# Turning more activations with transposing transfers instead of TensorE, in a two-layer hybrid encoder on one core

## The chip, the cores and the metric

The kernel runs on one core of a Trainium2 chip. The metric is the device time of one execution in microseconds (us). Three runs of the kernel before took 907.43, 908.38 and 909.86 us; the median is 908.38 us. The profile comes from a further execution, which took 909.68 us.

## The reference

The program is an encoder trunk of two layers for one sequence of 256 tokens and a width of 1024, in float32. Each layer projects the normalized input once and feeds two branches; their gated sum goes through an output projection, a SwiGLU feed-forward block and a per-layer embedding. Cut to what matters here:

```python
def hybrid_layer(h, p_i, ...):
    u = rms_norm(h, g_mix_pre)
    (gq, gk, gv, gg, ra_f, ra_b, aq, ak, av, gate_a, gate_b) = jnp.split(u @ w_in, offsets, axis=-1)
    ...                                       # gated linear attention, both directions
    o_gla = rms_norm(o_f + o_b, g_gla_out).reshape(b, s, GLA_VAL)
    branch_a = (o_gla * jax.nn.silu(gg)) @ w_o_gla          # the gated outputs
    q = apply_axial_rope(rms_norm(aq.reshape(b, s, ATTN_HEADS, HEAD_DIM), g_q_norm), cos, sin)
    k = apply_axial_rope(rms_norm(ak.reshape(b, s, ATTN_KV_HEADS, HEAD_DIM), g_k_norm), cos, sin)
    branch_b = gqa_attention(q, k, v) @ w_o_attn            # 8 query heads in 2 groups
    mixed = jax.nn.sigmoid(gate_a) * branch_a + jax.nn.sigmoid(gate_b) * branch_b   # the mix
    h = h + rms_norm(mixed @ w_out, g_mix_post)
    gate, up = jnp.split(rms_norm(h, g_ffn_pre) @ w_ffn_in, 2, axis=-1)
    h = h + rms_norm((jax.nn.silu(gate) * up) @ w_ffn_out, g_ffn_post)              # hidden: 2816
    e = p_i @ w_ple_proj
    return h + rms_norm(jax.nn.sigmoid(h @ w_ple_gate) * e, g_ple_post)
```

## The kernel before

**Products in three passes.** Every float32 operand of a product is kept as a high part and a low part in the type fp32r, and a product is three passes on TensorE (PE): high by high, low by high, high by low. `split` makes the parts: a CAST on ScalarE (ACT) for the high part, a subtraction on VectorE (DVE) for the low part (both are line 134 of the profile).

**Weights.** They stream from HBM by transfers that SyncE (SP) issues, 1 MB at a time into a `raw` or `lent` buffer. ACT casts each to `wh` in two pieces of 128x1024, DVE makes `wl` from `raw` and `wh`, and PE reads the two. A raw buffer is free for the next load when DVE is through with it.

**Activations.** The tokens stand in two halves of 128 (`hf`). A result that is the next product's contracted operand has to be turned, 128x128 at a time. There are two ways to do it.

- `transpose_in` (and, with code of its own, the queries' loop in `attend`, line 1267): PE transposes four blocks against `ident` into a bank of PSUM (`aux`), then `split` reads the bank. The profile shows these transposes as matmuls of 128x128 with `ident`.
- `turn_out` and `take_in`: ACT copies a 128x512 float32 tile as 16-bit words, the low and the high words apart (line 468), SP issues a transposing transfer of the words (DMA_TRANSPOSE, line 469), and ACT copies the turned words together again (line 476), after which `split` reads them from SBUF. The kernel before does this for all hidden blocks of the feed-forward block but the last pair, nine transfers per layer.

**The order.** Work beside the main run of products is written as generators in a `Task`. Each `yield n` asks to be called again after n ticks, and each half of a projection's product is a tick. `WAIT_MIX`, `W["g"]` and `WAIT_TURNED` are such counts. Inside `tc.high_priority(AHEAD)` instructions are placed ahead of their place in the code, as early as their operands allow. Each engine then works its own list in order: an instruction that waits holds up all behind it on its engine.

**Where the turned tiles occur.** In `attend(g)` for g = 0 and g = 1 each half of the queries (`qrs`, in the profile `mid_0rq` and `mid_1rq`, the digit being the layer) is transposed, scores against the keys follow, then softmax. The keys' parts lie in `big_0kv` and are made by the same casts and subtractions. In `out_gate` the gated outputs (`mid_0gg`) become `gT` (`big_0gg`). In `merge` the sum of the gated branches (`big_0gate`, by half `hf` and column half `j`) becomes `mixT` (`big_0merge`), read by the product with `w_out` (`acc_0wout`). `turn_in`, used by `out_gate`, makes a task that calls `transpose_in` twice for each half.

Of the kernel before, what the change touches and what calls it, by code (L numbers as in the profile page):

```python
# [13 lines left out]
U16 = mybir.dt.uint16  # L14
# [4 lines left out]
P = 128  # L19
T = 256  # L20
# [12 lines left out]
W = dict(r=5, z=6, s0=4, s=3, s1=9, o0=1, o=1, k=4, q=3, a0=1, a1=4, a2=4, a3=1, g=6)  # L33

STEPS_FIRST = "00 10 01 11 02 12 03 13".split()
STEPS = "00 01 02 10 03 11 12 13".split()
# [24 lines left out]
def trunk_kernel(ctx: ExitStack, tc: tile.TileContext, a: dict, out: bass.AP):  # L61
# [7 lines left out]
    nc = tc.nc  # L69
# [11 lines left out]
    part = ["start"]  # L81
# [8 lines left out]
    def mid(dt=F32):  # L90
        return b4p.tile([P, 1024], dt, tag="mid", name=nm("mid"))
# [4 lines left out]
    def aux():  # L96
        return accp.tile([P, 512], F32, tag="acc", name=nm("aux"))
# [34 lines left out]
    def split(hi, lo, src):  # L132

        return nc.scalar.copy(hi, src), nc.vector.tensor_tensor(out=lo, in0=src, in1=hi.bitcast(F32), op=ALU.subtract)  # L134


    h = cp.tile([P, 2, D], F32, tag="h", name="h")
# [24 lines left out]
    ident = cp.tile([P, P], F32, tag="ident", name="ident")  # L162
# [282 lines left out]
    def transpose_in(sp, src, k, n, hf, plain=None):  # L445

        ps = aux()
        for i in range(n):
            nc.tensor.transpose(ps[:, i * P : (i + 1) * P], src[:, i * P : (i + 1) * P], ident)
        with tc.high_priority(AHEAD):  # L450
            sp.put(ps[:, : n * P], k, n, hf * P, P)
        if plain is not None:
            nc.scalar.copy(plain, ps[:, : n * P])

    def turn_out(src, k, hf):

        with tc.high_priority(AHEAD):
            both, turned = halves(mid())
            turned = turned.bitcast(U16)
            parts = both.bitcast(U16).rearrange("p (s c) -> p s c", s=2)  # L460
            words = src.bitcast(U16)
            if hf is None:
                nc.scalar.copy(
                    parts.rearrange("p s (k h f) -> p s k h f", k=2, f=P),
                    words.rearrange("p (h k f s) -> p s k h f", h=2, f=P, s=2),
                )
            else:
                nc.scalar.copy(parts, words.rearrange("p (c s) -> p s c", s=2))
            nc.sync.dma_start_transpose(out=turned.rearrange("p (x t) -> p x t", t=P), in_=parts.rearrange("p s c -> p (s c)"))
        return both, turned  # L470

    def take_in(sp, both, turned, k, hf):

        n, tn = (2, T) if hf is None else (4, P)
        hi, lo = sp.at(k, n, (hf or 0) * P, tn)
        nc.scalar.copy(
            both.bitcast(U16).rearrange("p (k t s) -> p k t s", s=2, t=tn),
            turned.rearrange("p (s k t) -> p k t s", s=2, t=tn),
        )
        split(hi, lo, both.rearrange("p (k t) -> p k t", t=tn))  # L480

    last_pow = [None]

# [62 lines left out]
    def halves(t):  # L546
        return [t[:, j * 512 : (j + 1) * 512] for j in range(2)]

    def turn_in(sp, x, hf, wait, plain=None, apart=False):


        def turn():
            yield wait
            for j, y in enumerate(halves(x)):
                if j and apart:
                    yield 1
                transpose_in(sp, y, 4 * j, 4, hf, plain and plain[j])

        sp.makers[hf].append(Task(turn(), part[0]))
# [489 lines left out]
    for l in range(DEPTH):  # L1049
# [58 lines left out]
        qrs, qss, ranks = [], [], []  # L1108
# [50 lines left out]
        o = {}  # L1159
# [100 lines left out]
        def attend(g):  # L1260
            qs = []
            for hf in range(2):
                yield W["q"]
                ps = aux()
                for i in range(4):
                    hd = 4 * g + i
                    nc.tensor.transpose(ps[:, i * P : (i + 1) * P], qrs[hf][:, hd * P : (hd + 1) * P], ident)
                qh, ql = halves(mid(F32R))
                split(qh, ql, ps)
# [173 lines left out]
        gg = big().rearrange("p (s c) -> p s c", s=2)  # L1443
        for j in range(2):
            o = project(uT)
# [69 lines left out]
        def merge(br):  # L1515
            def then(j, hf, o):
                sl = [s[:, hf, j * 512 : (j + 1) * 512] for s in sgate[: br + 1]]
                vmul(sl[br], o, sl[br])
                if br == 1:
                    nc.vector.tensor_tensor(out=sl[0], in0=sl[0], in1=sl[1], op=ALU.add)  # L1520
# [46 lines left out]


        part[0] = f"{l}ffnin"
        hid = Split()  # L1570
        us = [[ws.take() for _ in range(2)] for _ in range(2)]

        def turned(src, k, hf):

            def turn():
                if k == 2 * PAIRS[-1]:
                    yield WAIT_LAST[hf]
                    transpose_in(hid, src, k, 4, hf)
                else:
                    x = turn_out(src, k, hf)  # L1580
                    yield WAIT_TURNED
                    take_in(hid, *x, k, hf)
# [193 lines left out]
```

## Time and profile before

| | |
|---|---|
| runs, us | 907.43, 908.38, 909.86 |
| profiled execution, us | 909.68 |
| its span, us | 907.9 |
| PE busy | 898.8 us, 99% |
| DVE busy | 790.2 us, 87% |
| ACT busy | 620.5 us, 68% |
| POOL busy | 105.9 us, 12% |
| weights' queue (q1) | 177.25 MB, 59.9% of the 16 DMA engines' span |
| clock granted to PE | 0.999 |

The span is what lies between the first and the last instruction of the profile; 1.8 us of the profiled execution's own time lie outside it. In a timeline row the first number is the start in us from the span's start, the second the time from the first start to the last end of a group, and a bracket at the end names idle time of the engine ahead of the group and what ended it. In rows of groups by line, three durations in ns are the least, the median and the longest. Times of single rows below are of this one execution.

### The profile page before, as it was taken

To read this page: it belongs to the slowest core of one execution; us is meant where nothing else is said; L and a number is where in the kernel's file an instruction comes from. 1 tells how busy PE (TensorE), PEld (TensorE's weight loads), DVE (VectorE), ACT (ScalarE), POOL (GpSimd) and SP (SyncE) were. 2 spreads that over 40 slices of the span, in tenths; PEclk is the share of its full clock that TensorE was granted. 3 is DMA by queue.
4 is the path that set the end of the run, shared out by engine and by line. 5 is a ranking of instruction groups with operands and counts; after the bars stand their busy time and mean duration, and the time that the engine had idled before them with its cause. 6 is when DMAs were issued, how large, how long until landed. Compare 5 with 4: busy or idle time off the path is not lost.

```text
span 907.9 us, 12157 instructions
## 1 busy us (share of the span) xinstructions
PE 898.8 (99%) x4479; PEld 762.2 (84%) x4479; DVE 790.2 (87%) x1021; ACT 620.5 (68%) x1011; POOL 105.9 (12%) x157
## 2 busy tenths in 40 slices
PE   9999999999999999999999999999999999999997
PEld 8898888888888887887898888888888888888886
DVE  7999989987668999998779899799876799999984
ACT  7688677564467787756676687675644796958563
POOL 3700221300100000000254001110000000000001
PEclk9999999999999999999999999999999999999999
DMA  8663445657397594956576424455573966858461
GB/s 283 219 189 136 140 140 191 216 187 249 115 288 204 173 301 146 317 170 233 180 279 204 168 93 140 139 186 185 186 241 100 309 180 206 254 210 264 150 231 47
DMA packets 108519, 178.16 MB, mean 196 GB/s; under 512 B 22494, under 2 KB 46566, under 8 KB 107948
## 3 DMA queue, kind: packets, MB, share of 16 engines
q1 hardware_dynamic: 108300, 177.25, 59.9%
q8 instruction: 35, 0.57, 0.3%
q14 instruction: 24, 0.20, 0.1%
q10 hardware_dynamic: 160, 0.14, 0.0%
HBM read 169.50 MB, written 3.15 MB: 190 GB/s over the span
## 4 chain that ended last, share of the span: by engine, by line
PE 78%; DVE 11%; DMA 4%; issue 4%; ACT 2%; POOL 0%; SPq 0%; POOLq 0%; ACTq 0%; DVEq 0%
PE acc_1ffnin L122 12%; PE acc_0gate L122 7%; PE acc_1gate L122 7%; PE acc_1ffnin L106 7%; DVE wl_0ffnin L134 6%; PE acc_1rq L122 3%; PE acc_0gqk L106 2%; PE acc_1gqk L106 2%; PE acc_1wout L122 2%; PE acc_0ple L122 2%; PE acc_1v L122 2%; PE acc_0gg L122 2%; PE acc_1gg L122 2%; PE acc_0v L122 2%; PE acc_0merge L122 2%
## 5 line engine op out<-in xcount | busy, mean ns | idle before, releaser
L134 ACT CAST wh_0ffnin<-raw_0ffnin 128x1024 fp32r<-128x1024 f32 x38 | 38.1, 1048 | 19.8 <-DMA raw_0ffnin<-in_w_ffn_out_dram 10.2
L134 ACT CAST wh_1ffnin<-raw_1ffnin 128x1024 fp32r<-128x1024 f32 x38 | 38.3, 1048 | 17.4 <-DMA raw_1ffnin<-in_w_ffn_out_dram 5.0
L134 DVE TENSOR_TENSOR wl_0ffnin<-raw_0ffnin,wh_0ffnin 128x1024 fp32r<-128x1024 f32 x38 | 44.6, 1219 | 5.8 <-ACT wh_0ffnin L134 5.8
L134 DVE TENSOR_TENSOR wl_1ffnin<-raw_1ffnin,wh_1ffnin 128x1024 fp32r<-128x1024 f32 x38 | 44.8, 1219 | 5.0 <-ACT wh_1ffnin L134 4.9
L106 PE MATMUL acc_0ffnin<-wh_0ffnin,big_0ffnin 128*128 128x512 f32 x176 | 45.4, 392 | 0.0
L106 PE MATMUL acc_1ffnin<-wh_1ffnin,big_1ffnin 128*128 128x512 f32 x176 | 45.1, 390 | 0.0
L122 PE MATMUL acc_0ffnin<-wh_0ffnin,big_0wout 128*128 128x512 f32 x168 | 41.8, 390 | 0.0
L122 PE MATMUL acc_1ffnin<-wh_1ffnin,big_1wout 128*128 128x512 f32 x168 | 41.5, 389 | 0.0
L106 PEld LDWEIGHTS acc_0ffnin<-wh_0ffnin,big_0ffnin 128*128 128x128 f32 x176 | 32.8, 188 | 7.5 <-DVE big_0ffnin L134 0.5
L106 PEld LDWEIGHTS acc_1ffnin<-wh_1ffnin,big_1ffnin 128*128 128x128 f32 x176 | 33.0, 188 | 6.9
L122 PEld LDWEIGHTS acc_0ffnin<-wh_0ffnin,big_0wout 128*128 128x128 f32 x168 | 31.4, 188 | 7.1 <-ACT wh_0ffnin L134 0.4
L122 PEld LDWEIGHTS acc_1ffnin<-wh_1ffnin,big_1wout 128*128 128x128 f32 x168 | 31.5, 188 | 6.5
L134 DVE TENSOR_TENSOR wl_1ffnin<-lent_1ffnin,wh_1ffnin 128x1024 fp32r<-128x1024 f32 x30 | 35.7, 1217 | 0.6 <-ACT wh_1ffnin L134 0.6
L134 DVE TENSOR_TENSOR wl_0ffnin<-lent_0ffnin,wh_0ffnin 128x1024 fp32r<-128x1024 f32 x30 | 35.6, 1216 | 0.1
L134 ACT CAST wh_1ffnin<-lent_1ffnin 128x1024 fp32r<-128x1024 f32 x30 | 30.7, 1051 | 5.4 <-PE acc_1ffnin L106 3.9
L134 ACT CAST wh_0ffnin<-lent_0ffnin 128x1024 fp32r<-128x1024 f32 x30 | 30.4, 1053 | 3.6 <-DVE lent_0ffnin L332 3.4
L134 ACT CAST wh_0gate<-raw_0gate 128x1024 fp32r<-128x1024 f32 x20 | 19.9, 1049 | 14.4 <-DMA raw_0gate<-in_w_o_attn_dram 6.1
L134 ACT CAST wh_1gate<-raw_1gate 128x1024 fp32r<-128x1024 f32 x20 | 19.9, 1048 | 13.9 <-PE acc_1gate L122 5.9
L134 DVE TENSOR_TENSOR wl_0gate<-raw_0gate,wh_0gate 128x1024 fp32r<-128x1024 f32 x20 | 24.2, 1257 | 5.2 <-ACT wh_0gate L134 5.1
L134 DVE TENSOR_TENSOR wl_1gate<-raw_1gate,wh_1gate 128x1024 fp32r<-128x1024 f32 x20 | 23.5, 1221 | 5.1 <-ACT wh_1gate L134 5.1
L106 PE MATMUL acc_0ffnin<-wl_0ffnin,big_0ffnin 128*128 128x512 f32 x88 | 24.6, 394 | 0.6 <-DVE wl_0ffnin L134 0.6
L106 PE MATMUL acc_1ffnin<-wl_1ffnin,big_1ffnin 128*128 128x512 f32 x88 | 24.0, 391 | 0.0
(730 smaller groups left out, 2731.7 us busy)
## 6 DMA issues: line engine op xcount, KB each, us to landing
raw_0ffnin<-in_w_ffn_out_dram SPq DMA_DIRECT2D x11, 1024.0 KB, 5.9
raw_1ffnin<-in_w_ffn_out_dram SPq DMA_DIRECT2D x11, 1024.0 KB, 5.5
lent_0ffnin<-in_w_ffn_in_dram SPq DMA_DIRECT2D x6, 1024.0 KB
lent_1ffnin<-in_w_ffn_in_dram SPq DMA_DIRECT2D x6, 1024.0 KB, 7.5
raw_0v<-in_w_in_dram SPq DMA_DIRECT2D x4, 1024.0 KB, 5.8
raw_0gate<-in_w_o_gla_dram SPq DMA_DIRECT2D x4, 1024.0 KB, 6.8
raw_0gate<-in_w_o_attn_dram SPq DMA_DIRECT2D x4, 1024.0 KB, 5.2
raw_0wout<-in_w_ffn_in_dram SPq DMA_DIRECT2D x8, 512.0 KB, 4.6
```

Source lines behind the costliest of these rows:

```text
L106: return nc.tensor.matmul(o, lhsT, rhs, start=start, stop=stop)
L122: nc.tensor.matmul(o, x, y, start=start and n == 0, stop=stop and n == len(seq) - 1, **kw)
L134: return nc.scalar.copy(hi, src), nc.vector.tensor_tensor(out=lo, in0=src, in1=hi.bitcast(F32), op=ALU.subtract)
```

## The change

Three more kinds of tile go the second way, in each of the two layers: the queries of the second group (g = 1; two tiles, 8 PE transposes), the gated outputs (four tiles, 16 transposes), and the mix apart from the tile of the second column half and first token half (three tiles of four, 12 of 16 transposes). So 36 PE transposes per layer go, and 9 transposing transfers with two ACT copies each come.

`turn_out` no longer takes a buffer of its own: one half buffer that is free by then (`parts`) takes the words apart, and the transfer writes the turned words back over the source. For the queries, `parts` is the half that held the first group's queries, so the first copy comes after that group's PE transposes. The transfer is issued outside `high_priority`, which holds for the feed-forward block's nine transfers per layer, too. The counts of ticks change: `WAIT_GATED` = 9, 11 replaces `W["g"]` = 6, and `WAIT_MIX` is counted by `j` and `hf`.

```diff
-WAIT_MIX = 3, 6
+WAIT_MIX = (5, 7), (3, 8)
...
+WAIT_GATED = 9, 11
...
-    def turn_out(src, k, hf):
+    def turn_out(src, parts, mixed=False):
         with tc.high_priority(AHEAD):
-            both, turned = halves(mid())
...
+            planes, words = (t.bitcast(U16) for t in (parts, src))
...
-                nc.scalar.copy(parts, words.rearrange("p (c s) -> p s c", s=2))
-            nc.sync.dma_start_transpose(out=turned.rearrange("p (x t) -> p x t", t=P), in_=parts.rearrange("p s c -> p (s c)"))
-        return both, turned
+                nc.scalar.copy(planes.rearrange("p (s c) -> p s c", s=2), words.rearrange("p (c s) -> p s c", s=2))
+        nc.sync.dma_start_transpose(out=words.rearrange("p (x t) -> p x t", t=P), in_=planes)
...
+                if g == 0:
+                    ps = aux()
+                    for i in range(4):
+                        nc.tensor.transpose(ps[:, i * P : (i + 1) * P], qrs[hf][:, i * P : (i + 1) * P], ident)
+                    split(qh, ql, ps)
+                else:
+                    take_in(*(t.rearrange("p (i t) -> p i t", t=P) for t in (qh, ql)), *halves(qrs[hf])[::-1])
...
                 prs.append(softmax(g, hf, qs[hf]))
+                if g == 0:
+                    turn_out(*halves(qrs[hf])[::-1])
...
-                turn_in(gT, sg, hf, W["g"])
+                xs = [(t, gg[:, hf, j * 512 : (j + 1) * 512]) for j, t in enumerate(halves(sg))]
+                for x in xs:
+                    turn_out(*x)
+                def turn(hf=hf, xs=xs):
+                    for j, x in enumerate(xs):
+                        yield WAIT_GATED[hf] if j == 0 else 1
+                        take_in(*gT.at(4 * j, 4, hf * P, P), *x)
...
                     def turn():
-                        yield WAIT_MIX[hf]
-                        transpose_in(mixT, sl[0], 4 * j, 4, hf)
+                        if (j, hf) != (1, 0):
+                            turn_out(*sl)
+                        yield WAIT_MIX[j][hf]
+                        if (j, hf) != (1, 0):
+                            take_in(*mixT.at(4 * j, 4, hf * P, P), *sl)
+                        else:
+                            transpose_in(mixT, sl[0], 4 * j, 4, hf)
```

In layer 0 the start of the attention shows what this does to ACT's list. `mid_0at` are the first group's queries, turned; `big_0kv` the keys; `wh_0kv` high parts of weights. Before:

```order
L134 CAST mid_0at_673<-aux_0at_668 128x512
L134 CAST wh_0kv_570<-raw_0rq_423 128x1024
L499 ACTIVATE big_0kv_539<-acc_0kv_541,rs_start_121 128x256
L1194 ACTIVATE t_0kv_610<-t_0kv_610,kss_0kv_611 128x128
L1194 ACTIVATE t_0kv_624<-t_0kv_624,kss_0kv_625 128x128
L1194 ACTIVATE t_0kv_610<-t_0kv_610,kss_0kv_611 128x128
L1194 ACTIVATE t_0kv_624<-t_0kv_624,kss_0kv_625 128x128
L134 CAST wh_0kv_570<-raw_0rq_423 128x1024
L134 CAST big_0kv_539<-aux_0kv_684 128x2x128
L134 CAST mid_0at_710<-aux_0at_705 128x512
L134 CAST big_0kv_539<-aux_0kv_713 128x2x128
```

The same stretch of ACT's list in the changed kernel:

```order
L466 COPY mid_0rq_161<-mid_0rq_161 128x1024
L135 CAST mid_0at_668<-aux_0at_669 128x512
L135 CAST wh_0kv_570<-raw_0rq_423 128x1024
L495 ACTIVATE big_0kv_539<-acc_0kv_541,rs_start_121 128x256
L1190 ACTIVATE t_0kv_610<-t_0kv_610,kss_0kv_611 128x128
L1190 ACTIVATE t_0kv_624<-t_0kv_624,kss_0kv_625 128x128 x2
L1190 ACTIVATE t_0kv_610<-t_0kv_610,kss_0kv_611 128x128
L135 CAST wh_0kv_570<-raw_0rq_423 128x1024
L466 COPY mid_0rq_163<-mid_0rq_163 128x1024
L135 CAST wh_0kv_602<-raw_0rq_528 128x1024 x2
L135 CAST big_0kv_539<-aux_0kv_684 128x2x128
L135 CAST mid_0at_705<-aux_0at_706 128x512
```

A first copy of words stands ahead of the first queries' cast, and a second copy and two casts of `wh_0kv_602` now stand ahead of both casts of the keys; before, the casts of `wh_0kv_602` followed the keys. The second cast of `big_0kv` is the next row after these.

On PE, the end of the first product block of `gqk` and the first scores (`aux_0at` out of `big_0kv` and `mid_0at`), before:

```order
L106 MATMUL acc_0gqk_642<-big_start_303,wh_0rq_522 128x512 x4
L106 MATMUL acc_0gqk_642<-big_start_303,wl_0rq_523 128x256 x4
L106 MATMUL aux_0at_727<-big_0kv_539,mid_0at_673 128x256
L106 MATMUL acc_0gqk_643<-big_start_303,wh_0rq_522 128x512
L106 MATMUL aux_0at_743<-big_0kv_539,mid_0at_673 128x256
L106 MATMUL acc_0gqk_643<-big_start_303,wh_0rq_522 128x512 x3
L106 MATMUL acc_0gqk_643<-big_start_303,wl_0rq_523 128x256 x4
```

And in the changed kernel:

```order
L107 MATMUL acc_0gqk_642<-big_start_303,wh_0rq_522 128x512 x4
L107 MATMUL acc_0gqk_642<-big_start_303,wl_0rq_523 128x256 x4
L107 MATMUL acc_0gqk_643<-big_start_303,wh_0rq_522 128x512 x4
L107 MATMUL acc_0gqk_643<-big_start_303,wl_0rq_523 128x256 x4
L107 MATMUL aux_0at_727<-big_0kv_539,mid_0at_668 128x256
L107 MATMUL aux_0at_743<-big_0kv_539,mid_0at_668 128x256
L107 MATMUL acc_0gqk_785<-big_start_149,wh_0kv_570 128x512 x2
```

The first two scores moved behind the eight matmuls into `acc_0gqk_643`.

At the end of the mix, ACT's list before (`big_0merge` is the turned mix, `aux_0merge` the PSUM bank that PE's transposes write):

```order
L134 CAST big_0merge_2215<-aux_0merge_2244 128x4x128
L134 CAST wh_0merge_2267<-raw_0merge_2188 128x1024 x2
L134 CAST big_0merge_2327<-aux_0merge_2322 128x4x128
L134 CAST mid_0wout_2301<-aux_0emb_2330 128x512
L524 ACTIVATE t_0wout_2377,ss_0wout_2375<-acc_0wout_2302 128x512
L134 CAST big_0merge_2327<-aux_0merge_2355 128x4x128
```

And in the changed kernel:

```order
L135 CAST big_0merge_2222<-big_0gate_2040 128x4x128
L135 CAST wh_0merge_2253<-raw_0merge_2180 128x1024 x2
L466 COPY big_0gate_2040<-big_0gate_1718 128x1024
L135 CAST big_0merge_2313<-aux_0merge_2308 128x4x128
L135 CAST mid_0wout_2287<-aux_0emb_2316 128x512
L472 COPY big_0gate_2040<-big_0gate_1718 128x1024
L135 CAST big_0merge_2313<-big_0gate_2040 128x4x128
```

The copy for the mix's last tile now stands between the casts of the weights and the cast of the one tile that PE still transposes.

More of the change, by code (lines that the diff above doesn't have):

```diff
@@ L30 @@
 WAIT_NEXT, WAIT_IN, WAIT_H = (7, 9), ((6, 9), (6, 6)), ((3, 5), (3, 5))
-WAIT_MIX = 3, 6
+WAIT_MIX = (5, 7), (3, 8)
 WAIT_SPREAD = 12
-W = dict(r=5, z=6, s0=4, s=3, s1=9, o0=1, o=1, k=4, q=3, a0=1, a1=4, a2=4, a3=1, g=6)
+W = dict(r=5, z=6, s0=4, s=3, s1=9, o0=1, o=1, k=4, q=3, a0=1, a1=4, a2=4, a3=1)
+WAIT_GATED = 9, 11
 STEPS_FIRST = "00 10 01 11 02 12 03 13".split()
@@ L453, in transpose_in @@
             nc.scalar.copy(plain, ps[:, : n * P])
-    def turn_out(src, k, hf):
+    def turn_out(src, parts, mixed=False):
         with tc.high_priority(AHEAD):
-            both, turned = halves(mid())
[L459 to L462, printed above, removed]
+            planes, words = (t.bitcast(U16) for t in (parts, src))
+            if mixed:
                 nc.scalar.copy(
-                    parts.rearrange("p s (k h f) -> p s k h f", k=2, f=P),
+                    planes.rearrange("p (s k h f) -> p s k h f", s=2, k=2, f=P),
                     words.rearrange("p (h k f s) -> p s k h f", h=2, f=P, s=2),
@@ L467, in turn_out, with take_in @@
             else:
-                nc.scalar.copy(parts, words.rearrange("p (c s) -> p s c", s=2))
-            nc.sync.dma_start_transpose(out=turned.rearrange("p (x t) -> p x t", t=P), in_=parts.rearrange("p s c -> p (s c)"))
-        return both, turned
-    def take_in(sp, both, turned, k, hf):
-        n, tn = (2, T) if hf is None else (4, P)
-        hi, lo = sp.at(k, n, (hf or 0) * P, tn)
+                nc.scalar.copy(planes.rearrange("p (s c) -> p s c", s=2), words.rearrange("p (c s) -> p s c", s=2))
+        nc.sync.dma_start_transpose(out=words.rearrange("p (x t) -> p x t", t=P), in_=planes)
+    def take_in(hi, lo, src, parts):
+        tn = hi.shape[-1]
         nc.scalar.copy(
-            both.bitcast(U16).rearrange("p (k t s) -> p k t s", s=2, t=tn),
-            turned.rearrange("p (s k t) -> p k t s", s=2, t=tn),
+            parts.bitcast(U16).rearrange("p (k t s) -> p k t s", s=2, t=tn),
+            src.bitcast(U16).rearrange("p (s k t) -> p k t s", s=2, t=tn),
         )
-        split(hi, lo, both.rearrange("p (k t) -> p k t", t=tn))
+        split(hi, lo, parts.rearrange("p (k t) -> p k t", t=tn))
     last_pow = [None]
@@ L1263, in attend @@
                 yield W["q"]
[L1264 to L1267, printed above, removed]
                 qh, ql = halves(mid(F32R))
-                split(qh, ql, ps)
+                if g == 0:
[5 more added lines that the diff above has]
+                    take_in(*(t.rearrange("p (i t) -> p i t", t=P) for t in (qh, ql)), *halves(qrs[hf])[::-1])
                 qs.append((qh, ql, qss[hf][:, 4 * g : 4 * g + 4]))
@@ L1461, in out_gate @@
                     vmul(t, t, on[:, hf, s])
-                turn_in(gT, sg, hf, W["g"])
+                xs = [(t, gg[:, hf, j * 512 : (j + 1) * 512]) for j, t in enumerate(halves(sg))]
[5 more added lines that the diff above has]
+                        take_in(*gT.at(4 * j, 4, hf * P, P), *x)
+                gT.makers[hf].append(Task(turn(), part[0]))
         ogate = Task(out_gate(), f"{l}gg")
@@ L1569, in trunk_kernel @@
         part[0] = f"{l}ffnin"
-        hid = Split()
+        hid, spare = Split(), []
         us = [[ws.take() for _ in range(2)] for _ in range(2)]
@@ L1579, in turn @@
                 else:
-                    x = turn_out(src, k, hf)
+                    if not spare:
+                        spare.extend(halves(mid()))
+                    parts = spare.pop()
+                    turn_out(src, parts, hf is None)
                     yield WAIT_TURNED
-                    take_in(hid, *x, k, hf)
+                    take_in(*(hid.at(k, 2, 0, T) if hf is None else hid.at(k, 4, hf * P, P)), src, parts)
             t = Task(turn(), part[0], k // 4)
```

## The prediction

> **What bounds the kernel now.** I read the page's busy times first, then the chain that ended last, then timelines at the places that the change touches. From the page:
>
> ```profile
> span 907.9 us, 12157 instructions
> PE 898.8 (99%) x4479; PEld 762.2 (84%) x4479; DVE 790.2 (87%) x1021; ACT 620.5 (68%) x1011; POOL 105.9 (12%) x157
> PE 78%; DVE 11%; DMA 4%; issue 4%; ACT 2%; POOL 0%; SPq 0%; POOLq 0%; ACTq 0%; DVEq 0%
> ```
>
> PE is busy for 99% of the span and carries 78% of the last chain. So a PE instruction that goes is time that goes, provided that no operand of a later one comes late. DVE's 87% warns that there are stretches in which its products (the low parts) arrive just in time; the windows show them for the stages concerned:
>
> ```profile
> core 0: us, PE busy (x) PEld busy (x) DVE busy (x) ACT busy (x) POOL busy (x), PEclk, DMA share, GB/s
> 45.00:100.00 55.00, 55.00 (x319) 48.08 (x318) 52.41 (x94) 45.39 (x95) 7.04 (x6) 1.00 0.45 148
> 147.00:201.00 54.00, 54.00 (x248) 44.95 (x247) 50.74 (x48) 33.91 (x41) 10.47 (x10) 1.00 0.52 176
> 248.00:300.00 52.00, 51.64 (x230) 41.49 (x229) 40.42 (x48) 38.61 (x58) 2.01 (x5) 1.00 0.80 232
> ```
>
> The first row is the attention's start in layer 0, the second the stage that takes the gated outputs, the third the start of the feed-forward block. PE never rests in the first two, while DVE is at 52.41 of 55 and 50.74 of 54 us, and ACT at 45.39 of 55. ACT has room on the whole, but little in the first.
>
> **What PE gets back.** Three of the removed sets, from PE's timeline; a row's own length holds the drain of its last matmul, so I count from its start to the next row's start:
>
> ```profile
> 97.22 0.60 PE L1267 MATMUL aux_0at<-ident,mid_0rq 128*128 128x128 f32 x4
> 97.57 0.71 PE L122 MATMUL acc_0v<-wh_0v,big_start 128*128 128x512 f32 x2
> ...
> 147.70 1.91 PE L449 MATMUL aux_0gg<-ident,mid_0gg 128*128 128x128 f32 x16
> 149.36 0.70 PE L122 MATMUL acc_0gate<-wh_0gg,big_start 128*128 128x512 f32 x2
> ...
> 216.12 0.60 PE L449 MATMUL aux_0merge<-ident,big_0gate 128*128 128x128 f32 x4
> 216.47 0.71 PE L122 MATMUL acc_0merge<-wh_0gate,big_0at 128*128 128x512 f32 x2
> ```
>
> Four transposes push PE back by 0.35 us, sixteen by 1.66. Per layer: 2 x 0.35 for the queries, 1.66 for the gated outputs, 3 x 0.35 for the mix, together 3.41 us; in two layers **-6.8 us**. That is the most that the change can give directly.
>
> **What ACT and SP get.** The feed-forward block shows the price of the new pieces:
>
> ```profile
> L468 ACT COPY mid_0ffnin<-t_0ffnin x6: 1038/1044/1047, 267.2 to 376.0; 128x1024 uint16<-128x1024 uint16 x6
> L476 ACT COPY mid_0ffnin<-mid_0ffnin x9: 1168/1177/1183, 274.0 to 380.8; 128x1024 uint16<-128x1024 uint16 x9
> L469 SPq DMA_TRANSPOSE mid_0ffnin<-mid_0ffnin x9: 1237/1250/1922, 268.3 to 377.1; - x9
> DMA to landing us min/median/max: 3.3/3.6/4.3
>   DMA mid_0ffnin<-mid_0ffnin: 12.0, 5
> ```
>
> A tile costs ACT 1.04 + 1.18 = 2.22 us, SP 1.25 us, and from issue to landing 3.6 us. Eighteen tiles add 40 us to ACT's 620.5, which makes 73% of the span. DVE keeps its subtractions. The last row says that in layer 0 ACT stood idle for 12.0 us in five waits for such landings. None of this costs time while the products of ACT keep ahead of PE; so I place the copies at each point by the order and compare with the rows.
>
> *Queries, layer 0.*
>
> ```profile
> 46.25 0.59 ACT L134 CAST mid_0at<-aux_0at 128x512 fp32r<-128x512 f32 x1 [1.27 <-PE aux_0at L1267]
> 49.23 1.04 ACT L134 CAST wh_0kv<-raw_0rq 128x1024 fp32r<-128x1024 f32 x1
> 51.58 0.38 ACT L134 CAST big_0kv<-aux_0kv 128x256 fp32r<-128x256 f32 x1
> 52.12 1.06 ACT L134 CAST wh_0kv<-raw_0rq 128x1024 fp32r<-128x1024 f32 x1
> ...
> 52.51 0.28 PE L106 MATMUL aux_0at<-big_0kv,mid_0at 128*128 128x256 f32 x1
> 54.17 1.08 PE L106 MATMUL acc_0gqk<-big_start,wh_0kv 128*128 128x512 f32 x4
> 69.46 1.32 PE L122 MATMUL acc_0v<-wh_0gqk,big_start 128*128 128x512 f32 x5
> 53.21 2.36 DVE L134 TENSOR_TENSOR wl_0kv<-raw_0rq,wh_0kv 128x1024 fp32r<-128x1024 f32 x2 [0.73 <-ACT wh_0kv L134]
> ```
>
> The keys are ready at 51.96 and wanted at 52.51, a lead of 0.55 us. In the changed list a copy (1.04) goes in at 46.25, so the cast of 49.23 ends at 51.3; then come the second copy (to 52.4), two weight casts (1.0 each, to 54.4), and the casts of keys, queries, keys (about 0.3, 0.5 and 0.4): the keys are ready at 55.5. PE meanwhile does the eight matmuls that moved ahead, and arrives at 54.17 less the two scores (some 0.1 each without the drain that a row of 0.28 holds), at 53.9. It waits 1.6 us. The bounds are 0, if a cast of weights finds its buffer taken and the real lists run otherwise than placed, and 2.5, if the low part of the keys, a subtraction that stands behind the two of `wl_0kv` (2.36 together) on DVE now, comes late on top. I take **+1.6**, since each row of the sum is in the trace. On SP two transfers now stand ahead of the next weights' load; it fills the buffer that the weights of row 69.46 (`wh_0gqk`) come from, 17 us after the keys are wanted, so 2 us of delay is covered.
>
> *Queries, layer 1.*
>
> ```profile
> 501.93 0.59 ACT L134 CAST mid_1at<-aux_1at 128x512 fp32r<-128x512 f32 x1 [0.76 <-PE aux_1at L1267]
> 506.76 0.59 ACT L134 CAST mid_1at<-aux_1at 128x512 fp32r<-128x512 f32 x1
> 507.25 0.38 ACT L134 CAST big_1kv<-aux_1kv 128x256 fp32r<-128x256 f32 x1
> ...
> 508.19 1.38 PE L106 MATMUL aux_1at<-big_1kv,mid_1at 128*128 128x256 f32 x9
> ```
>
> Here three copies stand ahead of the last keys: words apart for the first tile (ends 503.0), together again once its transfer has landed (503.0 + 3.6, then 1.18: 507.8), words apart for the second. With one activation, the queries' cast and the keys' own (about 0.4, 0.5 and 0.4, by the last two rows of ACT), the keys end near 510.1 instead of 507.63. PE arrives at 508.2, or 0.7 later by three 128x512 matmuls that moved ahead (0.23 each from start to start, by the mix's rows below): a wait of 1.2 to 1.9. I take **+1.2**, with 0 and 1.9 as bounds.
>
> *Gated outputs.* Eight copies per layer. The windows' second row gives ACT 20 us of room in 54, so the sum fits; the question is the order. The first casts of weights in this stage slip by some 4 us:
>
> ```profile
> 154.20 2.01 ACT L134 CAST wh_0gate<-big_0gate 128x1024 fp32r<-128x1024 f32 x2 [2.11 <-PE acc_0gate L122]
> 158.36 1.06 ACT L134 CAST wh_0gate<-raw_0gate 128x1024 fp32r<-128x1024 f32 x1
> 163.33 2.35 DVE L134 TENSOR_TENSOR wl_0gate<-raw_0gate,wh_0gate 128x1024 fp32r<-128x1024 f32 x2
> ...
> 167.60 1.07 PE L122 MATMUL acc_0gate<-wl_0gate,big_0gg 128*128 128x512 f32 x4
> ```
>
> The pair cast by 159.4 is subtracted at 163.33 and its low part wanted at 167.60. Placed by the order the cast ends near 165 and the low part near 166.7, and PE, 1.66 us earlier, wants its second half at 166.4. That is a tie. I take **+0.1** per layer, with 0 and 1.5 (the whole gain) as bounds.
>
> *Mix.*
>
> ```profile
> 225.08 2.00 ACT L134 CAST wh_0merge<-raw_0merge 128x1024 fp32r<-128x1024 f32 x2 [1.90 <-DMA raw_0merge<-in_w_out_dram]
> 228.59 0.59 ACT L134 CAST big_0merge<-aux_0merge 128x512 fp32r<-128x512 f32 x1 [1.51 <-PE aux_0merge L449]
> 227.59 0.69 DVE L1520 TENSOR_TENSOR big_0gate<-big_0gate,big_0gate 128x512 f32<-128x512 f32 x1
> 229.28 1.09 PE L122 MATMUL acc_0wout<-wl_0merge,big_0merge 128*128 128x512 f32 x4
> 230.21 0.40 PE L122 MATMUL acc_0wout<-wh_0merge,big_0merge 128*128 128x512 f32 x1
> ```
>
> The last copy cannot start before the addition ends at 228.28, so the cast behind it ends at 229.9 instead of 229.18, and the low part follows 0.7 later. PE wants them at 230.21 and two matmuls of 0.23 after (four take 0.93 from 229.28); without the first eight transposes that is 229.5 and 230.0. The wait is 0.4 to 0.6, nothing if the addition also comes earlier, and 1.3 if the weights ahead, whose loads now stand behind two transfers on SP, push the copy by 0.7 more. I take **+0.8** per layer.
>
> *Feed-forward block.* The moved transfers get up to one load later on SP's list, which can lengthen or shorten the 12.0 us of ACT's waits by a microsecond or so; the third window has PE short by only 0.36 of 52 us. I take 0, with -1 and +2.
>
> Sum: -6.8 + 1.6 + 1.2 + 2 x 0.1 + 2 x 0.8 = **-2.2 us**. The profiled execution's 909.68 us (its span of 907.9 and 1.8 around it) becomes 907.5; it was 1.3 us above the median of the runs, so on the runs' scale I forecast **906.2 us** against 908.38.
>
> On this very choice the Trainium skill has a rule in "VectorE: DVE Perf Modes", section "Rules for kernel authors": a 128x128 transpose belongs on TensorE where a PSUM destination will do, and on the transposing DMA otherwise. By that rule the change should not pay. The trace agrees on latency (3.6 us to land beside 1.66 for sixteen transposes), and the rule says nothing of a PE that is never idle; by the rule alone the sum would be the stalls without the gain, +4.6.
>
> **The rivals.** About 0.3% (2.7 us) is what a measurement of this kernel can tell from no change.
>
> *Cover holds.* The lists run so that none of the five stalls happens, since ACT has 27% to spare. For it speaks that every placing above is mine. Against it stand the leads of 0.55 us at the keys. It gives -6.8: 901.6. Chance 0.25.
>
> *The gain ends in the feed-forward block.* What PE wins in layer 0 is given back where the weights, not PE, set the pace: DVE has 11% of the last chain, and the third window has the DMA engines at 0.80. Half of the 2.2 us goes, 1.1, and the later transfers cost 1: 908.3. Against it, PE's idle time there is 0.36 us in 52. Chance 0.11.
>
> *Landings hold up ACT in the gated outputs' stage: slower.* There each half's two copies "together again" stand ahead of weight casts on ACT's list. If the first of each pair waits like those of the feed-forward block, 12.0/5 = 2.4 us, that is 4.8 per layer against about 1 us of lead: 3.8 per layer, 7.6 in all, -2.2 + 7.6 = +5.4: 913.8. It turns the sign beyond 1.1 us per layer and is measurable beyond 2.5. For it: five waits of nine in layer 0. Against: the transfers are issued 5 us and more ahead of those copies by my placing, and in layer 1 the trace has only
>
> ```profile
>   DMA mid_1ffnin<-mid_1ffnin: 3.2, 3
> ```
>
> Chance 0.22. The skill's rule above would point this way.
>
> **Chances.** The forecast has 0.42, with a range of its own of 904 to 908, half of it beyond the bound on the fast side. Faster: 0.25 + 0.21 = 0.46. Same: 0.21 + 0.09 = 0.30. Slower: 0.22 + 0.02 = 0.24. The range runs from 901.0 (cover holds, and 0.6 of the feed-forward block's 1) to 912.5, inside the slower rival.
>
> **What would show it.** Right: PE's busy time and span both fall by 2 to 3 us; PE waits of 1 to 2 us ahead of the first scores in both layers, for ACT's cast of `big_0kv`; one of 0.5 to 1 near the second column half of the mix; no wait at the gated outputs. Wrong: no PE gap at the scores (cover holds); gaps at `acc_0gate` for `wl_0gate`, with ACT waiting for landings of `big_0gg` (the slower rival); or more PE gaps than now in `acc_0ffnin`.

## The result and the profile after

The changed kernel takes 920.89 us (median of five runs, 918.53 to 923.13) against 908.38 (of five, 907.43 to 909.86); the ratio is 1.0133, 95% interval 1.0109 to 1.0157. It is slower by 12.5 us where 2.2 less were forecast, and outside the range. The trace after is of the fastest of the five executions (918.53 us), so it shows 8.7 us of the 12.5. From its page:

```profile
span 916.6 us, 12087 instructions
PE 895.1 (98%) x4407; PEld 757.0 (83%) x4407; DVE 791.2 (86%) x1021; ACT 656.1 (72%) x1047; POOL 103.0 (11%) x157
PE 57%; DVE 22%; DMA 8%; ACT 7%; issue 5%; POOL 1%; POOLq 0%; ACTq 0%; DVEq 0%; SPq 0%
```

PE has 72 matmuls fewer and is busy for 3.7 us less, and the span is 8.7 us longer. The chain that ended last leaves PE: 78% before, 57% now, with DVE doubled and ACT and DMA at 15% together. ACT rose by 35.6 us, near the 40 that were worked out, and DVE hardly at all; no engine became the bound. The time is in waits. From the list of waits, the largest of PE's own rows (total us, times, longest); the last row is the largest that the kernel before had behind its first few microseconds:

```profile
PE acc_1wout L123 <- ACT big_1merge L135: 3.3, 2, 2.9
PE aux_1at L107 <- ACT big_1kv L135: 2.1, 1, 2.1
PE aux_0merge L450 <- DVE big_0gate L1529: 1.6, 1, 1.6
PE acc_0ffnin L107 <- DVE wl_0ffnin L135: 1.6, 4, 0.5
PE acc_0wout L123 <- ACT big_0merge L135: 1.4, 1, 1.4
PE aux_1merge L450 <- DVE big_1gate L1529: 1.3, 1, 1.3
PE aux_0at L107 <- ACT big_0kv L135: 1.1, 1, 1.1
```

```profile
PE acc_0ffnin L106 <- DVE wl_0ffnin L134: 0.6, 2, 0.3
```

Four rows are the mix (7.6 us), two the first scores (3.2), one the feed-forward block. The rows left out are of 0.4 us and less, apart from 1.0 at the program's start, which the kernel before has too. None belongs to the gated outputs' stage. A wait costs more than its row, since the first matmul behind it starts slower: counted from PE's starts, wherever a step exceeds the median step of its shape by over 0.15 us, the excess adds up to 2.7 us before and 17.5 after. Less the 6.8 us of transposes that is +8.0 of the 8.7.

The first scores in layer 0, on ACT, DVE and PE:

```profile
54.81 0.37 ACT L135 CAST big_0kv<-aux_0kv 128x256 fp32r<-128x256 f32 x1
55.55 0.38 ACT L135 CAST big_0kv<-aux_0kv 128x256 fp32r<-128x256 f32 x1
54.00 2.36 DVE L135 TENSOR_TENSOR wl_0kv<-raw_0rq,wh_0kv 128x1024 fp32r<-128x1024 f32 x2 [0.67 <-ACT wh_0kv L135]
56.28 0.42 DVE L135 TENSOR_TENSOR big_0kv<-aux_0kv,big_0kv 128x256 fp32r<-128x256 f32 x1
55.99 0.38 PE L107 MATMUL aux_0at<-big_0kv,mid_0at 128*128 128x256 f32 x1 [1.08 <-ACT big_0kv L135]
56.75 0.39 PE L107 MATMUL aux_0at<-big_0kv,mid_0at 128*128 128x256 f32 x1 [0.38 <-DVE big_0kv L135]
57.35 0.73 PE L107 MATMUL acc_0gqk<-big_start,wh_0kv 128*128 128x512 f32 x2 [0.21 <-DVE mid_0at L135]
```

The keys are ready at 55.93; 55.5 was placed. PE waits 1.08 us for the high part and then, as the upper bound had it, for the low part behind the two subtractions of `wl_0kv`. In layer 1:

```profile
513.16 1.17 ACT L472 COPY mid_1rq<-mid_1rq 128x1024 uint16<-128x1024 uint16 x1 [2.04 <-DMA mid_1rq<-mid_1rq]
515.92 0.39 ACT L135 CAST big_1kv<-aux_1kv 128x256 fp32r<-128x256 f32 x1
516.36 0.50 PE L107 MATMUL aux_1at<-big_1kv,mid_1at 128*128 128x256 f32 x2 [2.11 <-ACT big_1kv L135]
```

The transfer, issued at 508.21, took 4.9 us instead of 3.6; ACT stood for 2.04 us, with the keys' cast behind it.

The mix in layer 0 (DVE, ACT, SP, PE; the first row of PE is its first product with `w_out`):

```profile
227.49 2.36 DVE L135 TENSOR_TENSOR wl_0merge<-raw_0merge,wh_0merge 128x1024 fp32r<-128x1024 f32 x2 [0.76 <-ACT wh_0merge L135]
230.18 0.69 DVE L135 TENSOR_TENSOR big_0merge<-big_0gate,big_0merge 128x512 fp32r<-128x512 f32 x1 [0.33 <-ACT big_0merge L135]
230.79 0.68 DVE L1529 TENSOR_TENSOR big_0gate<-big_0gate,big_0gate 128x512 f32<-128x512 f32 x1
231.99 1.22 DVE L135 TENSOR_TENSOR wl_0merge<-raw_0merge,wh_0merge 128x1024 fp32r<-128x1024 f32 x1
233.12 0.68 DVE L1529 TENSOR_TENSOR big_0gate<-big_0gate,big_0gate 128x512 f32<-128x512 f32 x1
...
230.33 1.99 ACT L135 CAST wh_0merge<-raw_0merge 128x1024 fp32r<-128x1024 f32 x2 [0.19 <-DMA raw_0merge<-in_w_out_dram]
233.84 1.04 ACT L466 COPY big_0gate<-big_0gate 128x1024 uint16<-128x1024 uint16 x1 [1.51 <-DVE big_0gate L1529]
234.79 0.58 ACT L135 CAST big_0merge<-aux_0merge 128x512 fp32r<-128x512 f32 x1
...
224.98 0.37 SPq L298 DMA_DIRECT2D raw_0merge<-in_w_out_dram  x1
...
225.46 0.50 PE L123 MATMUL acc_0wout<-wh_0merge,big_0merge 128*128 128x512 f32 x1
231.53 0.66 PE L450 MATMUL aux_0merge<-ident,big_0gate 128*128 128x128 f32 x4 [1.65 <-DVE big_0gate L1529]
235.42 0.51 PE L123 MATMUL acc_0wout<-wh_0merge,big_0merge 128*128 128x512 f32 x1 [1.41 <-ACT big_0merge L135]
```

The same places in the kernel before (DVE, SP, PE):

```profile
224.66 0.68 DVE L134 TENSOR_TENSOR big_0merge<-aux_0merge,big_0merge 128x512 fp32r<-128x512 f32 x1
225.25 0.68 DVE L1520 TENSOR_TENSOR big_0gate<-big_0gate,big_0gate 128x512 f32<-128x512 f32 x1
...
220.09 0.37 SPq L297 DMA_DIRECT2D raw_0merge<-in_w_out_dram  x1
...
223.87 0.39 PE L122 MATMUL acc_0wout<-wh_0merge,big_0merge 128*128 128x512 f32 x1
```

Two new waits follow one another. The addition at 230.79, which PE's transposes need, stands on DVE's list behind a low part (230.18), as it did before (224.66, 225.25); but this low part now has to wait for a copy and a cast on ACT. Then ACT itself stands 1.51 us ahead of the last copy, until the second addition (233.12) is through, and the urgent cast, whose operand lies ready in PSUM, stands behind that copy. In layer 1 the same step costs 2.86 us.

The weights have come late, too. The last load of `w_out` was issued 3.8 us ahead of PE's first product with `w_out` before (220.09 and 223.87), and 0.5 us ahead of it now. ACT's casts of these weights begin 4.9 us behind that product (230.33), where they began 1.2 us behind it (225.08 in the prediction's rows), and the second addition stands on DVE's list behind a low part of these weights (231.99).

### The profile page after: what moved, and what is told of

Read it like the earlier page. It is cut to its first block, busy times and chain, and to the rows that moved or that the text cites. A ratio compares the mean times of both kernels' runs of the same rounds, so it can differ in the third digit from the quotient of the medians.

```text
span 916.6 us, 12087 instructions
## 1 busy us (share of the span) xinstructions
PE 895.1 (98%) x4407; PEld 757.0 (83%) x4407; DVE 791.2 (86%) x1021; ACT 656.1 (72%) x1047; POOL 103.0 (11%) x157
## 4 chain that ended last, share of the span: by engine, by line
PE 57%; DVE 22%; DMA 8%; ACT 7%; issue 5%; POOL 1%; POOLq 0%; ACTq 0%; DVEq 0%; SPq 0%
PE acc_1ffnin L123 12%; PE acc_1ffnin L107 7%; PE acc_0ffnin L123 5%; DVE wl_0ffnin L135 5%; DVE wl_0gate L135 3%; DVE wl_1gate L135 3%; PE acc_1rq L123 3%; PE acc_0ple L123 2%; PE acc_1v L123 2%; PE acc_0ffnin L107 2%; PE acc_1ple L123 2%; PE acc_0gg L123 2%; PE acc_1gg L123 2%; PE acc_1wout L123 2%; PE acc_0wout L123 2%
## 5 line engine op out<-in xcount | busy, mean ns | idle before, releaser
L135 DVE TENSOR_TENSOR wl_0ffnin<-lent_0ffnin,wh_0ffnin 128x1024 fp32r<-128x1024 f32 x30 | 35.6, 1217 | 1.5 <-ACT wh_0ffnin L135 1.5
L135 ACT CAST wh_1gate<-raw_1gate 128x1024 fp32r<-128x1024 f32 x20 | 19.8, 1050 | 11.9 <-DMA raw_1gate<-in_w_o_attn_dram 7.3
```

## The experiments

Theory A says that PE waits because the copies on ACT, and what DVE does behind them, stand in front of urgent work in lists worked in order. Theory B says that the transfers at normal priority, issued later, spoil the feed-forward block. Times below are medians less the median of the kernel before on the same chip.

**The parts alone.** In each kernel the other parts go back to TensorE, with their old counts of ticks; the transfers stay at normal priority. The lines that each such edit adds, apart from what it removes:

```diff
                 # queries, in both groups
+                ps = aux()
+                for i in range(4):
+                    hd = 4 * g + i
+                    nc.tensor.transpose(ps[:, i * P : (i + 1) * P], qrs[hf][:, hd * P : (hd + 1) * P], ident)
+                split(qh, ql, ps)
                 # gated outputs
+                turn_in(gT, sg, hf, 6)
                     # mix
+                        yield (3, 6)[hf]
+                        transpose_in(mixT, sl[0], 4 * j, 4, hf)
```

`e1_ffn_only` takes all three back. 

> Queries, gated outputs and mix are turned by TensorE as before; what is left of the change is that the feed-forward block's transfers are issued at normal priority and write back over their source. Theory A (the loss is PE waiting for operands that ACT's copies and DVE's queue make late at the scores and in the mix): within 1.5 us of before, about +0.5. Theory B (the transfers that moved behind loads on SP's list spoil the feed-forward block): most of the loss, +6 us or more.

Measured: +1.9 us (911.91 against 909.98; ratio 1.0024, 1.0007 to 1.0041). Not nothing, but a sixth of the loss.

`e2_queries` keeps the queries. 

> Only the second group's queries go by transfers (and what e1_ffn_only holds). Theory A: PE gains 1.4 us and loses the waits seen at the first scores in the changed kernel, about 3.0 us in layer 0 and 2.3 in layer 1, and up to 1.7 us by the lower clock after the first: +4 to +6 us against before. Theory B: as e1_ffn_only, less 1.4. The prediction's own terms: +1.4.

Measured: +4.4 us (914.35; 1.0051, 1.0033 to 1.0070), 2.4 over e1_ffn_only. In layer 1 the wait is far smaller than in the whole change:

```profile
509.35 1.18 ACT L472 COPY mid_1rq<-mid_1rq 128x1024 uint16<-128x1024 uint16 x1 [0.27 <-DMA mid_1rq<-mid_1rq]
512.56 0.51 PE L107 MATMUL aux_1at<-big_1kv,mid_1at 128*128 128x256 f32 x2 [0.34 <-ACT big_1kv L135]
```

The order is the same, but the transfer, issued at 506.17, lands after 3.2 us instead of 4.9.

`e3_gated` keeps the gated outputs. 

> Only the gated outputs go by transfers (and what e1_ffn_only holds). Theory A: no PE wait in this stage, so -3.3 us and what e1_ffn_only costs: -2 to -3.5 against before. Theory B: +3 or more.

Measured: +0.5 us (910.50; 1.0009, 0.9994 to 1.0025), 1.4 below e1_ffn_only. The sign of A, half its size.

`e4_mix` keeps the mix. 

> Only 12 of the mix's 16 blocks go by transfers (and what e1_ffn_only holds). Theory A: PE gains 2.1 us and loses the waits seen in the changed kernel, 3.5 us in layer 0 and 5.1 in layer 1: +6.5 against before, more where the clock falls. Theory B: as e1_ffn_only, less 2.1. The prediction's own terms: -0.5.

Measured: +7.0 us (916.99; 1.0068, 1.0044 to 1.0091), 5.1 over e1_ffn_only. The mix is the dear part. Its trace is of the fastest execution (912.39; the other four took 916.07 to 917.90), so it shows less than the median holds.

**The priority of the transfers.** One edit puts the transfer back under the high priority:

```diff
-        nc.sync.dma_start_transpose(out=words.rearrange("p (x t) -> p x t", t=P), in_=planes)
+            nc.sync.dma_start_transpose(out=words.rearrange("p (x t) -> p x t", t=P), in_=planes)
```

`e5_gated_hi` is e3_gated with it. 

> As e3_gated, but the transfers are issued inside the high priority again, those of the feed-forward block too. If the normal priority costs what e1_ffn_only showed (+1.9 us), this is 2 us below e3_gated: -1 to -2 us against before. If the feed-forward block takes its pace from the weights whatever PE wins ahead of it, it stays within 1 us of before.

Measured: -2.6 us (906.86 against 909.49; 0.9971, 0.9960 to 0.9982), the only version that beats the kernel before. On SP's list six transfers of the feed-forward blocks go one weight load ahead again; besides them only one small load of constants moves. The time to landing (least, median, longest) of those transfers for which the trace tells it, six of 26 in e3_gated and then four of 26 in e5_gated_hi:

```profile
DMA to landing us min/median/max: 3.1/4.3/6.5
```

```profile
DMA to landing us min/median/max: 3.1/3.2/3.4
```

The three long ones in e3_gated (5.2, 6.2 and 6.5 us) are of the six that went behind one more load; the other three took 3.1 to 3.4. ACT waits for such a transfer in order, and PE's waits for low parts in the feed-forward blocks add up to 3.5 us in e3_gated's trace and to 1.2 in e5_gated_hi's. At the place where sixteen transposes stood, PE goes on at once:

```profile
146.72 1.07 PE L123 MATMUL acc_0gate<-wl_0gg,big_start 128*128 128x512 f32 x4
147.63 1.98 PE L123 MATMUL acc_0gate<-wh_0gg,big_start 128*128 128x512 f32 x8
```

`e8_all_hi` is the whole change with that edit. 

> The whole change, but all transposing transfers are issued inside the high priority. Theory A (copies on ACT and DVE's in-order lists at the scores and in the mix): still slower by 8 us or more, since the copies stand where they stood. Theory B (the normal priority): back within 3 us of before.

Measured: +9.3 us (918.80; 1.0100, 1.0069 to 1.0131). By the medians B explains some 3 us of the loss; the other 9 stay where the copies stay, as A has it.

**Inside the mix.** `e9_mix_j0` is e4_mix with two tiles instead of three; the counts of ticks stay those of the change.

```diff
-                        if (j, hf) != (1, 0):
+                        if j == 0:
                             turn_out(*sl)
```

> Mix alone, with only the first column half's two tiles by transfers (8 of 16 blocks): the copy ahead of the urgent cast of the tile that TensorE still turns is gone. PE gains 1.4 us. Theory A: the wait ahead of the second half's products (2.1 and 2.0 us in the trace of e4_mix) goes: 3 to 6 us below e4_mix, that is +1 to +3 against before. If the wait came from the weights' loads behind the transfers, it stays within 1.5 us of e4_mix.

Measured: +3.9 us (913.43; 1.0038, 1.0019 to 1.0058), 3.1 below e4_mix. The waits at the urgent cast, in e4_mix (both layers) and then what e9_mix_j0 has at the mix's end in layer 0:

```profile
231.42 0.50 PE L123 MATMUL acc_0wout<-wh_0merge,big_0merge 128*128 128x512 f32 x1 [1.93 <-ACT big_0merge L135]
685.42 0.51 PE L123 MATMUL acc_1wout<-wh_1merge,big_1merge 128*128 128x512 f32 x1 [1.83 <-ACT big_1merge L135]
```

```profile
229.69 0.66 PE L450 MATMUL aux_0merge<-ident,big_0gate 128*128 128x128 f32 x4 [1.32 <-DVE big_0gate L1516]
232.38 0.50 PE L123 MATMUL acc_0wout<-wh_0merge,big_0merge 128*128 128x512 f32 x1 [0.21 <-ACT big_0merge L135]
```

Without the last tile's copy the wait for the cast falls from 1.93 to 0.21 us, and in layer 1 from 1.83 to none. In layer 1 neither trace has another wait of PE in the mix, so there it is shown that the copy ahead of the cast made it. In layer 0 it is not: e9_mix_j0 waits for DVE's addition instead, which e4_mix's trace does not, and for 0.61 us at the first product, so its waits there add up to 2.1 us against 1.9.

`e6_mix_late` leaves the copy and moves the low part.

```diff
-WAIT_MIX = (5, 7), (3, 8)
+WAIT_MIX = (5, 11), (3, 8)
```

> As e4_mix, but the second token half of the first column half is taken in later (11 ticks instead of 7): its low part no longer stands on DVE's list ahead of the additions that the second column half waits for. Theory A (DVE's order and the copy ahead of the urgent cast make the mix late): the wait of 2.0 us per layer in e4_mix's trace falls to about 1: 1.5 to 3 us below e4_mix, +3.5 to +5 against before. If the copy alone, or the weights' loads, set that wait, it stays within 1 us of e4_mix.

Measured: +2.7 us (913.43 against 910.73; 1.0042, 1.0026 to 1.0059), a larger gain than expected, yet its trace still has 2.00 and 1.48 us at the urgent cast. On ACT in layer 0:

```profile
228.04 2.00 ACT L135 CAST wh_0merge<-raw_0merge 128x1024 fp32r<-128x1024 f32 x2 [2.08 <-DMA raw_0merge<-in_w_out_dram]
229.94 1.04 ACT L466 COPY big_0gate<-big_0gate 128x1024 uint16<-128x1024 uint16 x1
```

The copy no longer waits for an addition; ACT waits for the last load of `w_out` instead, and the copy and the urgent cast follow. So the low part's place did not set that wait by itself: with it out of the way, the load and the copy made the same wait. The weights' loads were the other cause that was named ahead of the run. What the median gained over e4_mix lies in e4_mix's longer executions, of which there is no trace.

`e7_gated_hi_mix` is e5_gated_hi with the mix's twelve blocks. 

> The whole change without the queries, transfers inside the high priority. If the parts add up, the mix costs on top of e5_gated_hi what it costs on top of e1_ffn_only, about +5 us: +2 to +3 against before. If earlier transfers are what the mix lacked, within 1 us of e5_gated_hi.

Measured: +2.6 us (913.30 against 910.73; 1.0024, 1.0004 to 1.0043), 5.2 over e5_gated_hi by the differences to before: the mix costs the same with early transfers.

`e14_gated_hi_mix_late` is e5_gated_hi with only the mix's tiles of the second token half, their copies and transfers outside the high priority, and with `WAIT_MIX = (3, 11), (3, 9)`.

```diff
-                        if (j, hf) != (1, 0):
-                            turn_out(*sl)
+                        if hf == 1:
+                            turn_out(*sl, ahead=hf == 0)
```

> e5_gated_hi and, in the mix, only the two tiles of the second token half by transfers, the last one's copy at normal priority and so no longer far ahead of the urgent cast. Per layer PE gains 0.7 us more. Theory A: the urgent cast still follows one copy, and one low part still stands ahead of the additions: the gain is eaten, 0 to +2 us against e5_gated_hi. If the waits go: -1.4 against e5_gated_hi, 904.5 on the first scale.

Measured: +1.3 us (911.31 against 910.03; 1.0017, 1.0006 to 1.0029), 3.9 over e5_gated_hi, worse than expected. The copy still stood ahead of the urgent cast, now with one cast of weights between them, and PE waited there for 1.43 and 1.78 us; in layer 0 ACT had stood 2.02 us for the load of these weights.

**The queries' copies.** `e10_queries_late` is e2_queries with the copies of words apart at normal priority.

```diff
-                    turn_out(*halves(qrs[hf])[::-1])
+                    turn_out(*halves(qrs[hf])[::-1], ahead=False)
```

> Queries alone, with ACT's copies of the words apart at normal priority: in layer 0 the keys' casts come before the second copy and the weight casts again. Theory A: the wait at layer 0's first scores falls from some 2.4 us to under 0.5 and the clock stays up: +1 to +2 us against before instead of +4.4. Theory B: as e2_queries.

Measured: +4.0 us (913.49 against 909.49; 1.0042, 1.0027 to 1.0057), hardly better than e2_queries and more than the +1 to +2 of A. The wait at layer 0's first scores is gone, as A had it, but a new one stands at the second group's scores, whose queries now come late:

```profile
100.73 1.33 PE L107 MATMUL aux_0at<-big_0kv,mid_0at 128*128 128x256 f32 x9 [1.60 <-DVE mid_0at L135]
```

**Together.** `e12_again` is the changed kernel once more. 

> The changed kernel, unaltered, on the chip of these runs. If the parts add up, what e1 to e4 showed: 1.9 + 2.4 (queries) - 1.4 (gated outputs) + 5.1 (mix) = +8 us. If the first comparison's +12.5 holds, some 4 us come from the parts being together.

Measured: +12.2 us (922.95 against 910.73; 1.0125, 1.0088 to 1.0162). The parts' 8 us are 4 short. `e13_gated_queries_hi` is e8_all_hi without the mix. 

> The whole change without the mix, transfers inside the high priority. If the parts add up: e5_gated_hi (-2.6) and the queries (+2.4 on top of e1_ffn_only): within 1 us of before. If the queries are dearer in company (in the changed kernel the transfer at layer 1's scores takes 4.9 us to land, in e2_queries 3.2, and the clock falls after the wait): +3 or more, with a wait of about 2 us at layer 1's first scores.

Measured: +0.5 us (910.49 against 910.03; 1.0000, 0.9987 to 1.0013): these two add up, and its transfer at layer 1's scores lands in 3.2 us. It takes queries and mix together to make 4 us more, that is e8_all_hi's 9.3 against 0.5 here and some 5 for the mix. These 4 us are a difference of several medians and not far beyond their noise: the interval of e8_all_hi alone runs from +6.3 to +11.9 us. Two things go with it: the later landing in layer 1 (4.9 us, ACT's wait there 2.0 to 2.2 us in all three traces of the whole change), and the clock. The changed kernel around its first scores, by stretches of 5 us:

```profile
core 0: us, PE busy (x) PEld busy (x) DVE busy (x) ACT busy (x) POOL busy (x), PEclk, DMA share, GB/s
50.00:55.00 5.00, 4.91 (x32) 4.17 (x30) 4.08 (x5) 5.00 (x9) 0.00 (x0) 1.00 0.54 125
55.00:60.00 5.00, 3.42 (x15) 2.94 (x16) 4.31 (x9) 4.48 (x10) 0.00 (x0) 0.81 0.99 316
60.00:65.00 5.00, 5.00 (x29) 4.46 (x28) 4.09 (x10) 5.00 (x12) 0.00 (x0) 0.85 0.45 153
```

And e8_all_hi behind layer 1's first scores and its mix:

```profile
515.00:520.00 5.00, 5.00 (x26) 4.73 (x27) 2.98 (x9) 2.98 (x6) 0.00 (x0) 0.69 0.48 74
695.00:700.00 5.00, 5.00 (x17) 3.93 (x16) 0.46 (x1) 2.34 (x4) 0.00 (x0) 0.66 0.92 261
```

After the waits the granted clock falls for a few microseconds: 5 x 0.19 + 5 x 0.15 = 1.7 us in the first case, about 1.6 and 1.7 in the others. In stretches of 1 us the first fall reads 0.56, 0.50, 0.50 and 0.74 (58 to 62 us), so it is a halving of some 3.4 us. The three traces of the whole change have one, two and three such falls (the changed kernel, e12_again, e8_all_hi); the kernel before and the versions with fewer parts have none in their traces, apart from the last 6 us of each. What the mean clock lacks to 1, times the span, is 5.0, 3.7 and 4.6 us on average over the executions of the same three, and some 1.6 us in the kernel before; so an estimate is that the clock makes 2 to 3 us of the whole loss. In e2_queries it is 1.8 us, in e4_mix 2.2 and in e13_gated_queries_hi 3.1, so the clock makes a part of the 4 us, too. No run took the clock's fall away by itself, so this share is counted, not shown. A third thing that the parts share is the lead of the last load of `w_out` on PE's first product with it, in layer 0 3.8 us before, 1.8 in e5_gated_hi, 2.4 in e4_mix and 0.5 in the change; no run tests what it is worth. Why the same transfer lands later when the mix is turned by transfers, too, stays open.

## Why the prediction was wrong

**The gain on PE** was right as a gross figure: where sixteen transposes stood, the next matmul follows, and PE's busy time fell by 3.7 us, though slow restarts behind its waits and the 1.7 us of lower clock lengthen it.

**Mix: the step that failed.** It was put at +0.8 us of waiting per layer, 0 to 1.3, against 1.05 of gain: -0.5 in all. The runs showed about +5 (e4_mix over e1_ffn_only, e7_gated_hi_mix over e5_gated_hi). I placed ACT's copy at the addition's time of the trace before and checked where it left the cast, but took that time as given, and for late weights I allowed 0.7 us, as the upper bound. The low parts that stand ahead of the additions on DVE's list, as they did before, now wait for copies on ACT; and the last load of `w_out` is issued 3.3 us later, counted from PE's first product with it, right behind the low part that DVE ends at 224.95 in the trace after. So the addition ended late (233.80), the copy waited for it, and the cast waited behind the copy. e9_mix_j0 shows the link from the copy to the cast in layer 1; e6_mix_late shows that without the late addition the late load makes the same wait, with the copy behind it. How the price divides between the two stays open, since no run moved the loads alone. The place was foreseen; the chain through two engines and the loads was not.

**Normal priority: the second.** Put at 0, bounded by -1 and +2; e1_ffn_only showed +1.9, and e3_gated against e5_gated_hi 3.1 by the differences to before. I took the landing as 3.6 us wherever the transfer was issued; that is the median of the four of 18 transfers for which the trace before tells it. Three that went behind one more load took 5.2 to 6.5 in e3_gated's trace.

**Queries** were near in the sum, in part by luck: +1.4 (1.6 + 1.2 - 1.4), 2.4 over e1_ffn_only alone. In e2_queries's trace PE waits 1.7 us at layer 0's first scores, the low part among them, which I had as the bound, and 0.3 in layer 1, where I had put 1.2. The medians' difference is larger than these rows, and no row accounts for the rest. In the whole change layer 1's wait is 2.11, beyond the bound of 1.9, with the transfer at 4.9 us. What I left out was the company of the mix, worth another 4 us or so.

**Gated outputs** were right in mechanism: the list of waits after has none there (e3_gated's has one of 0.3 us, for weights), so the slower rival that I put there, landings that hold up ACT, did not happen. The net -3.1 came out as -2.6 at most (e5_gated_hi). The rival that did happen on the slow side has its place in the mix, and its price is larger than the whole gain.

**The rule of the Trainium skill** ("VectorE: DVE Perf Modes" of the Trainium skill, section "Rules for kernel authors": TensorE for a 128x128 transpose if PSUM will do) held for queries and mix: their 40 transposes took 3.5 us, and the waits in their places in the trace after take 10.8. It did not hold for the gated outputs, wanted some 18 us behind the transposes (147.70 in the prediction's rows; PE's first product with `big_0gg` starts at 165.79 in the trace before): there e5_gated_hi is faster by 2.6 us.

## What to carry to other kernels

Work taken off a full engine is worth its price only where its replacement is not on the list in front of something urgent: look at what stands behind each new instruction on its engine, and then at what that one feeds on the next engine, one round further than seems needed. When a step's lead is half a microsecond, count every list it passes through, not only the one that was edited, and the loads that those lists release. A transfer whose landing an engine waits for in order should be issued ahead of bulk loads: that was worth 3 us here, near half of what all 72 transposes took.

## What the runs showed of the hardware

A transposing transfer of 128x1024 16-bit words landed 3.1 to 3.4 us after its issue in e5_gated_hi's trace (four that the trace tells of), and after 5.2 to 6.5 us in e3_gated's for three that went behind one more weight load. A load close ahead does not always delay it (one of the four was issued 1.7 us behind a load and landed in 3.4), and the transfer at layer 1's scores took 4.9 us in the changed kernel though the last load had been issued 6.9 us ahead of it. The granted clock fell to 0.50 for some 3.4 us behind some waits; those at layer 0's first scores add up to 1.7 us (1.08, 0.38 and 0.21 above). It does not fall behind every wait: the 2.86 us that end at 694.56 in the trace after are followed by a stretch at 1.00 (695 to 700 us). "TensorE: Matmul & The Clock Gate" of the Trainium skill (Part 1) gives half rate after an idle window of about 3.4 us. The half rate agrees with the 0.50; no wait here was that long, so as far as idle time goes the measured falls come sooner than the page has it.
